# Five plain opening blocks for four, weights split ahead during the output product, and attention stacks in one step

## The chip, the cores and the metric

The kernel runs on one core of a Trainium2 chip, in one launch. The metric is device time in microseconds (us); a run's time is that of one execution, and a kernel's the median of its runs. The engines are called PE (TensorE, matmuls), DVE (VectorE), ACT (ScalarE), POOL (GpSimd) and SP (SyncE, which here issues the DMAs).

## The reference

An encoder trunk on x of 512 tokens by 1024 features, float32, two layers. Each layer is SwiGLU, a token mixer, SwiGLU, every one between two RMS norms:

```python
def swiglu(h, w_in, w_out):
    g, u = jnp.split(h @ w_in, 2, axis=-1)      # 1024 -> 2 x 2816
    return (jax.nn.silu(g) * u) @ w_out         # 2816 -> 1024

for layer in range(2):
    h = swiglu(rms_norm(x, g[0]), ffn_w_in[layer, 0], ffn_w_out[layer, 0])
    x = x + 0.5 * rms_norm(h, g[1])
    h = token_mixer(rms_norm(x, g[2]), ...)     # proj = h @ w_in; 8 attention heads of 64, 4 mLSTM heads of 128
    x = x + rms_norm(h, g[3])                   # mixer output: concat(heads) @ w_out
    h = swiglu(rms_norm(x, g[4]), ffn_w_in[layer, 1], ffn_w_out[layer, 1])
    x = x + 0.5 * rms_norm(h, g[5])
```

## The kernel before

All matmuls keep float32 accuracy with three products: each operand is a rounded part hi and a rest lo, and `hi*hi + hi*lo + lo*hi` is summed. Activations and weights are both split: ACT casts hi (L97, L114, L297), DVE subtracts to get lo (L99, L115, L299). Weights arrive by DMAs of 512 KB on SP's queue into a ring `raw` of three tiles; `hi` and `lo` are rings of three as well. A further set of numbered slots, reused over the whole program, holds activations and temporary tiles (`chunk(name, slot)`): 11 to 16 the tq pairs, 17 and 19 first the two xf tiles and later the loads `wu`, 18, 20 and 21 the weight sums `ws`.

**An FFN's input product** (`ffn_in`) goes over 22 column blocks f of 128. The first `ne` = 4 are plain openings, `block(f, left)` for tokens 0 to 255 and then `block(f, right)` for tokens 256 to 511, each loading and splitting the weights of g and u anew. So PE can work on the left half while the right half of the activations is still made. Then `xx.finish()` makes the last combined operand: it reads the tile xf in slot 17 and writes it split into the right half of xh and xl (L228 on ACT, L229 on DVE). From then on `seven(f)` computes a block for both halves with seven products in place of eight (Strassen-Winograd). It needs sums of weight quarters: `Weights(f)` loads g into the raw ring and u into slot 17 or 19 (`wu`, 17 + 2 * (f % 2); for f = ne + 1 the raw ring), DVE makes the sums (L320 to L323), ACT and DVE split them (L297, L299). PE's tiles there are pa, pb, pc.

**An output product** (`out_half`, for FFN and mixer) runs for tokens 0 to 255 and then 256 to 511 into tiles o; `whole` drives it. The FFN has 22 loads of weights in each half, the mixer 8. The last two blocks of a half are kept to its end. Behind each half, `chain(t)` follows for its two tiles of 128 tokens: `post` (L160; norm of the product and residual), `pre` (L174; next norm, nt at L185), PE transposes (tr, L191), the split into xh (L209) and xl (L210), and for an FFN the copies and sums that become xf and tq (L236 to L245, L228, L229). The powers for the norms are on POOL (L136). The chain of tokens 256 to 511 thus runs beside the start of the next stage.

**The mixer** begins with four groups of natural projections (`proj_nat`) on tiles 0 and 1, then transposed projections (`mixer_proj_T`), the groups again on tiles 2 and 3, gates, mLSTM, and attention. Attention takes 32 steps of scores (sc), softmax (sm) and transposes (pt); `stack_pair` puts a pair of heads into the layout that the scores need (PE stk, then kst, qsh and qsl by ACT and DVE), in two steps. It is paced with the first half of the output product.

Inside an engine, instructions run in program order; a scheduler that knows the dependences sets that order at build time from the order of the code. In the FFN's seven-product part the order is as written. The numbers behind tile names below are buffer numbers and only tell tiles of one name apart.

Of the kernel before, what the change touches and what calls it, by code (L numbers as in the profile page):

```python
# [18 lines left out]
P = 128  # L19
# [22 lines left out]
def trunk_kernel(ctx, tc, x, norm_gain, ffn_w_in, ffn_w_out, mix_w_in, conv_w, conv_b,  # L42
# [50 lines left out]

    def halves_of(src, n, after=None):
# [3 lines left out]
        with tc.issue_after(after) if after else nullcontext():  # L98
            V.tensor_tensor(lo[:, :n], src, hi[:, :n].bitcast(F32), ALU.subtract)  # L99
        return [[w[:, q: q + 512].rearrange("p (k c) -> p k c", k=4) for w in (hi, lo)] for q in range(0, n, 512)]  # L100

    def split_w(load, n, k4, pieces=1):
        raw = raw_tile()
        hi = wp.tile([P, 1056], F32R, tag="hi", name="hi", bufs=3)
        lo = wp.tile([P, 1056], F32R, tag="lo", name="lo", bufs=3)
        m = n * k4

        def view(w):
            return w[:, :m].rearrange("p (k c) -> p k c", k=k4)
        step = k4 // pieces  # L110
        for k in range(0, k4, step):
            r, h, l = [view(w)[:, k: k + step] for w in (raw, hi, lo)]
            load(r, k)
            A.copy(h, r)  # L114
            V.tensor_tensor(l, r, h.bitcast(F32), ALU.subtract)  # L115
        return view(hi), view(lo)
# [54 lines left out]

    first_nt = []

    def pre(t, xn, xx, ps_of):  # L174
        ss = small("pre_ss", 2)
        opening = len(first_nt) < 2
        if opening:
            V.tensor_tensor_reduce(out=xn[:, 512:1024], in0=xs[:, t, 512:1024], in1=xs[:, t, 512:1024], op0=ALU.mult,
                                   op1=ALU.add, scale=1.0, scalar=0.0, accum_out=ss[:, 1:2])
        for n in range(1 if opening else 2):  # L180
            A.activation(junk, xs[:, t, n * 512: n * 512 + 512], AF.Square, accum_out=ss[:, n: n + 1])
        r = rsqrt_sum((ss[:, 0:1], ss[:, 1:2]), D, EPS, "i")
        for hf in range(2):
            c = slice(hf * 512, hf * 512 + 512)
            V.scalar_tensor_tensor(xn[:, c], xs[:, t, c], r, gpre[:, c], ALU.mult, ALU.mult)  # L185
            if opening and hf:
                first_nt.append(last_ins(mybir.EngineType.DVE))
            ps = ps_of("tr")
            for k in range(4):
                kk = hf * 4 + k  # L190
                PE.transpose(ps[:, k * P: (k + 1) * P], xn[:, kk * P: (kk + 1) * P], ident)  # L191
            xx.put(t, hf, ps.rearrange("p (k c) -> p k c", k=4))
# [59 lines left out]
    def product(ps, w, x, start):  # L252
        (wh, wl), (xh, xl) = w, x
        for k in range(4):
            PE.matmul(ps, wh[:, k], xh[:, k], start=start and k == 0, stop=False, skip_group_check=True)  # L255
            PE.matmul(ps, wh[:, k], xl[:, k], start=False, stop=False, skip_group_check=True)  # L256
            PE.matmul(ps, wl[:, k], xh[:, k], start=False, stop=k == 3, skip_group_check=True)  # L257

    ps_even, ps_odd = banks_of(0, 1, 2), banks_of(4, 5, 6)

    def ffn_in(layer, j, xx, late=None):
        w = ffn_w_in[layer, j].rearrange("(k p) c -> p k c", p=P)
# [18 lines left out]

        def block(f, c, pieces=1, after=None):
            h = h_of(f) if hts[f] is None else hts[f]
            banks = []
            for gu in range(2):
                lo_k, hi_k = halves_of(load(f, gu, pieces, True)[:, :1024], 1024, after)
                ps = psA("gu")[:, c]
                for q, w2 in enumerate((lo_k, hi_k)):
                    product(ps, w2, [x[:, 4 * q: 4 * q + 4, c] for x in (xx.h, xx.l)], q == 0)
                banks.append(ps)  # L290
            sil = t2("sil", f % 2)[:, c]
            A.activation(sil, banks[0], AF.Silu)
            V.tensor_tensor(h[:, c], banks[1], sil, ALU.mult)
# [89 lines left out]

        ne = 4
        for f in range(ne):
            block(f, left, 2 if late and f == 0 else 1, first_nt[-1] if late and f == 0 else None)
            if late and f < 2:
                late[f]()
        for f in range(ne):
            block(f, right)  # L390
# [48 lines left out]

    def whole(gen):  # L440
        banks = next(gen)
        run(gen)
        return banks

    def ffn_out(layer, j, hts, last):
        w = ffn_w_out[layer, j]

        def lhs_of(half):
            def go(f, idx):
                src = hts[f][:, half * 256: half * 256 + 256]  # L450
# [6 lines left out]
        return [lambda h=h: whole(out_half(w, NF, range(NF), lhs_of(h), (psA, psB)[h], last and h == 1)) for h in range(2)]  # L457

# [25 lines left out]

    def proj_nat(layer, xx, col, n, evac, tiles=range(NT), ps_of=None, per=1):
        xh, xl = xx.h, xx.l
        w = mix_w_in[layer].rearrange("(k p) c -> p k c", p=P)
        parts = []
        for q in range(2):
            def load(dst, _, q=q):  # L490
                nc.sync.dma_start(dst, w[:, q * 4: q * 4 + 4, col: col + n])
            parts.append(split_w(load, n, 4))
        for t0 in tiles[::per]:
            ps = (ps_of or psA)("nat")
            for u in range(per):
                tok = slice((t0 + u) * P, (t0 + u + 1) * P)
                d = ps[:, u * n: (u + 1) * n]
                for k in range(NK):
                    wh, wl = parts[k // 4]
                    PE.matmul(d, xh[:, k, tok], wh[:, k % 4], start=k == 0, stop=False)  # L500
                    PE.matmul(d, xh[:, k, tok], wl[:, k % 4], start=False, stop=False)  # L501
                    PE.matmul(d, xl[:, k, tok], wh[:, k % 4], start=False, stop=k == NK - 1)  # L502
                    if k == 3:
                        yield
                if u == per - 1:
                    evac(t0, ps)
                yield
# [21 lines left out]

    def mixer(layer, xx):  # L530
        cwr = t2("cwr", 5)
# [40 lines left out]
        groups = ((3336, 264, evac_mo(1)), (2560, 256, evac_mv(0)), (2816, 256, evac_mv(1)), (3072, 264, evac_mo(0)))  # L572
        for n, g in enumerate(groups):
            run(proj_nat(layer, xx, *g, tiles=(0, 1), per=1 + (n in (1, 2))))
        qk = mixer_proj_T(layer, cvt, xx)
# [3 lines left out]
        for n, g in enumerate(groups[1:]):  # L579
            run(proj_nat(layer, xx, *g, tiles=(2, 3), per=1 + (n < 2)))  # L580
            if n == 1:
                with tc.issue_after(last_ins(mybir.EngineType.PE)):
                    gates = next(gates)
# [37 lines left out]
        def stack_pair(hp):  # L621
            base = (20, 4)[hp % 2]
            ks = pair("kst", base)
            stack(kn, hp, ks, None)
            yield
# [4 lines left out]
            yield  # L630

# [21 lines left out]
        def opening():  # L653
            for n, _ in enumerate(heads()):
                if n == 58:
                    run(stack_pair(0))
                if n in (60, 64):
# [6 lines left out]
        def lhs_of(half):  # L664
            def go(f, idx):
# [170 lines left out]
    def stack(src, hp, dh, dl):  # L836
# [9 lines left out]
        else:  # L846
            for e, s, o in ((0, lo, hi), (1, hi, lo)):
                A.copy(dh[s, e], ps[s])
                A.copy(dh[o, e], ps[s])
                V.tensor_tensor(dl[s, e], ps[s], dh[s, e].bitcast(F32), ALU.subtract)  # L850
                A.copy(dl[o, e], dl[s, e].bitcast(F32))

    def attention(stack_pair, stacks, pts, av, mask, mm):
# [157 lines left out]
```

## Time and profile before

| | |
|---|---|
| runs | 2122.14 us median of 3 (2122.1 to 2124.03) |
| profiled execution | 2122.1 us, its span 2120.1 us, granted TensorE clock 0.982 on average |
| busy PE / DVE / ACT / POOL | 2041.7 / 1544.4 / 1154.5 / 253.6 us |
| DMA | 270 MB, 127 GB/s on average |

The span is the time from the first to the last instruction. Busy time of PE is the union of its matmuls; a matmul begins before the last one has ended, so its own duration is longer than its cost. "Idle before" and the waits name what ended an engine's idle time.

### The profile page before, as it was taken

What the parts mean: (1) busy time and instruction counts of PE and PEld (TensorE: products, weight loads), DVE (VectorE), ACT (ScalarE), POOL (GpSimd) and SP (SyncE); (2) the same over time, 40 slices, a digit from 0 to 9 for tenths busy, and PEclk for the clock granted to TensorE, in tenths of its full rate; (3) what the DMA queues carried; (4) which work ended last, traced back from release to release, by engine and by line L of the source; (5) the groups of instructions that cost most, each with busy time, mean ns of one, the idle gap of its engine ahead of it and who ended that gap; (6) DMA issues with size and microseconds to landing.
All of it is one profiled execution on the core that took longest, in us unless ns stands there. A gap on an engine that the chain in (4) does not pass through costs nothing. (4 is left out here: it accounts for less than half of the span.)

```text
span 2120.1 us, 35561 instructions
## 1 busy us (share of the span) xinstructions
PE 2041.7 (96%) x13870; PEld 1861.2 (88%) x13870; DVE 1544.4 (73%) x2634; ACT 1154.5 (54%) x2058; POOL 253.6 (12%) x330
## 2 busy tenths in 40 slices
PE   8899999999999989999998999999999999899998
PEld 7899988889977889998898999888899779899886
DVE  7688757685767878876687886667856677788665
ACT  5455555445665645555554555554456755455554
POOL 1000001233512100000010000003434220000000
PEclk9999999999999999999999999999999999999999
DMA  7433355541113633335663334564411235333364
GB/s 217 123 111 100 110 188 193 143 122 58 53 51 119 190 110 107 113 102 187 188 188 107 105 100 129 188 192 126 119 53 41 88 122 160 110 104 115 120 205 144
DMA packets 297566, 270.28 MB, mean 127 GB/s; under 512 B 8661, under 2 KB 267189, under 8 KB 297398
## 3 DMA queue, kind: packets, MB, share of 16 engines
q1 hardware_dynamic: 297398, 268.01, 41.8%
q8 instruction: 108, 1.77, 0.3%
q14 instruction: 60, 0.49, 0.1%
HBM read 265.88 MB, written 2.10 MB: 126 GB/s over the span
## 5 line engine op out<-in xcount | busy, mean ns | idle before, releaser
L115 DVE TENSOR_TENSOR lo<-raw,hi 128x1024 fp32r<-128x1024 f32 (+1 forms) x280 | 348.8, 1246 | 241.4 <-ACT hi L114 241.3
L114 ACT CAST hi<-raw 128x1024 fp32r<-128x1024 f32 (+1 forms) x280 | 294.5, 1053 | 311.0 <-PE o L419 225.6
L417 PE MATMUL o<-lo,hq 128*128 128x512 f32 x704 | 236.9, 394 | 0.8 <-DVE lo L115 0.8
L419 PE MATMUL o<-hi,hq 128*128 128x512 f32 x704 | 223.3, 394 | 0.0
L416 PE MATMUL o<-hi,hq 128*128 128x512 f32 x704 | 210.6, 395 | 2.5 <-ACT hq L453 2.5
L297 ACT CAST hi<-ws 128x1024 fp32r<-128x1024 f32 x144 | 151.2, 1052 | 70.9 <-ACT a L297 62.1
L255 PE MATMUL pa<-tq,hi 128*128 128x256 f32 x576 | 164.6, 286 | 22.3 <-ACT hi L297 22.3
L500 PE MATMUL nat<-hi,xh 128*128 128x256 f32 (+1 forms) x640 | 184.9, 291 | 0.0
L501 PE MATMUL nat<-lo,xh 128*128 128x256 f32 (+1 forms) x640 | 182.0, 285 | 2.9 <-DVE lo L115 2.9
L502 PE MATMUL nat<-hi,xl 128*128 128x256 f32 (+1 forms) x640 | 181.6, 285 | 0.0
L299 DVE TENSOR_TENSOR lo<-ws,hi 128x1024 fp32r<-128x1024 f32 x144 | 175.2, 1219 | 1.5 <-ACT hi L297 1.5
L257 PE MATMUL pa<-tq,lo 128*128 128x256 f32 x576 | 165.0, 286 | 1.9 <-DVE lo L299 1.9
L256 PE MATMUL pa<-tq,hi 128*128 128x256 f32 x576 | 164.8, 286 | 0.0
L255 PE MATMUL pc<-xh,hi 128*128 128x256 f32 x576 | 163.6, 284 | 0.0
L257 PE MATMUL pc<-xh,lo 128*128 128x256 f32 x576 | 163.4, 284 | 0.0
L256 PE MATMUL pc<-xl,hi 128*128 128x256 f32 x576 | 163.4, 284 | 0.0
L416 PEld LDWEIGHTS o<-hi,hq 128*128 128x128 f32 x704 | 131.9, 188 | 34.0 <-ACT hq L453 3.4
L417 PEld LDWEIGHTS o<-lo,hq 128*128 128x128 f32 x704 | 131.9, 188 | 31.5 <-DVE lo L115 1.1
L419 PEld LDWEIGHTS o<-hi,hq 128*128 128x128 f32 x704 | 132.3, 188 | 30.8
L256 PE MATMUL gu<-xl,hi 128*128 128x256 f32 x512 | 147.4, 289 | 6.6 <-DVE xl L210 6.6
L255 PE MATMUL gu<-xh,hi 128*128 128x256 f32 x512 | 146.8, 290 | 4.6 <-ACT xf L236 3.7
L257 PE MATMUL gu<-xh,lo 128*128 128x256 f32 x512 | 146.3, 288 | 0.0
(242 smaller groups left out, 5660.3 us busy)
## 6 DMA issues: line engine op xcount, KB each, us to landing
raw<-in_ffn_w_out_dram SPq DMA_DIRECT2D x176, 512.0 KB, 3.5
raw<-in_ffn_w_in_dram SPq DMA_DIRECT2D x138, 512.0 KB, 3.9
wu<-in_ffn_w_in_dram SPq DMA_DIRECT2D x68, 512.0 KB, 4.0
raw<-in_mix_w_in_dram SPq DMA_DIRECT2D x56, 512.0 KB, 3.8
raw<-in_mix_w_out_dram SPq DMA_DIRECT2D x32, 512.0 KB, 3.7
raw<-in_mix_w_in_dram SPq DMA_DIRECT2D x16, 528.0 KB, 3.7
gpost<-in_norm_gain_dram SPq DMA_DIRECT2D x6, 512.0 KB, 5.9
gpre<-in_norm_gain_dram SPq DMA_DIRECT2D x5, 512.0 KB, 4.7
```

Of the source, the lines that this page charges most:

```text
L114: A.copy(h, r)
L115: V.tensor_tensor(l, r, h.bitcast(F32), ALU.subtract)
L255: PE.matmul(ps, wh[:, k], xh[:, k], start=start and k == 0, stop=False, skip_group_check=True)
L256: PE.matmul(ps, wh[:, k], xl[:, k], start=False, stop=False, skip_group_check=True)
L257: PE.matmul(ps, wl[:, k], xh[:, k], start=False, stop=k == 3, skip_group_check=True)
L299: V.tensor_tensor(lo, src, fp(hi), ALU.subtract)
L416: PE.matmul(banks[t][n], a, wh[:, n], start=first, stop=False)
L417: PE.matmul(banks[t][n], a, wl[:, n], start=False, stop=False)
L419: PE.matmul(banks[t][n], b, wh[:, n], start=False, stop=end)
L500: PE.matmul(d, xh[:, k, tok], wh[:, k % 4], start=k == 0, stop=False)
L501: PE.matmul(d, xh[:, k, tok], wl[:, k % 4], start=False, stop=False)
L502: PE.matmul(d, xl[:, k, tok], wh[:, k % 4], start=False, stop=k == NK - 1)
```

## The change

- `ffn_in` has five plain openings. The right pass goes backwards (4, 3, 2, 1, 0), and the split weights of f = 4 are kept from the left pass to the right pass, which saves one load and split of g and u. The first seven-product block is f = 5.
- `early_split` loads and splits weights of the next stage while the second half of an output product runs, into slots 11 to 16, 20 and 21, which are free then. Ahead of three of the four FFNs these are g and u of f = 0 and 1 (four splits), ahead of each mixer the two parts of column group 2560 (two splits): 16 in all. `whole` calls them at even distances.
- In the mixer's first four groups, group 2560 comes first, and the second lo of the three other groups is subtracted on POOL.
- `stack_pair` runs in one step, at score steps 3, 13 and 17 in place of 2/4, 9/11 and 16/18. The second half of qsl is made by DVE from PSUM, no longer copied by ACT.
- At the opening of the kernel both squares of a norm are on ACT, and the rule that put the second nt ahead of the first lo is gone.
- The second half of the gates is taken one group later in the code; the order of instructions around it is the same.

The program has 48 matmuls more (128x256 each), 12 fewer lo subtracts of weights on DVE in the FFN input products (without the early ones), and as many DMAs as before.

The first place is the end of the right pass in the third FFN, ACT. `sil` ends an opening block, `xh<-xf` is the finish, `a22` and `hi<-ws` are casts of wu and of the weight sums, `ha` and `sil` wait for PE. Before:

```order
L297 CAST hi_12127<-raw_12117 128x1024
L292 ACTIVATE sil_12112<-gu_12056 128x256
L228 CAST xh_10437<-xf_10439 128x4x256
L350 COPY ha_12149<-pa_12152 128x256
L297 CAST a22_12136<-wu_12119 128x512
```

Now:

```order
L320 ACTIVATE sil_12152<-gu_12096 128x256
L325 CAST hi_12232<-raw_12222 128x1024
L325 CAST hi_12235<-ws_12226 128x1024
L320 ACTIVATE sil_12217<-gu_12161 128x256
L219 CAST xh_10423<-xf_10425 128x4x256
L325 CAST hi_12238<-ws_12227 128x1024
L378 COPY ha_12253<-pa_12256 128x256
```

The first `hi<-ws` moved from behind the finish and the first pa to a place ahead of the finish, and the finish no longer stands ahead of anything that reads wu.

The second place is SP's queue during the second half of the first layer's mixer output product. `raw<-in_mix_w_out` are its own weights, `raw<-in_ffn_w_in` those of the FFN that follows. Before:

```order
L423 DMA raw_7383<-in_mix_w_out_dram 128x1024
L423 DMA raw_7401<-in_mix_w_out_dram 128x1024
L423 DMA raw_7419<-in_mix_w_out_dram 128x1024
L423 DMA raw_7437<-in_mix_w_out_dram 128x1024
L423 DMA raw_7455<-in_mix_w_out_dram 128x1024
L423 DMA raw_7473<-in_mix_w_out_dram 128x1024
L423 DMA raw_7491<-in_mix_w_out_dram 128x1024
L423 DMA raw_7497<-in_mix_w_out_dram 128x1024
L272 DMA raw_7648<-in_ffn_w_in_dram 128x8x128
```

Now:

```order
L451 DMA raw_7376<-in_mix_w_out_dram 128x1024
L451 DMA raw_7394<-in_mix_w_out_dram 128x1024
L267 DMA raw_7412<-in_ffn_w_in_dram 128x8x128
L451 DMA raw_7418<-in_mix_w_out_dram 128x1024
L451 DMA raw_7436<-in_mix_w_out_dram 128x1024
L267 DMA raw_7448<-in_ffn_w_in_dram 128x8x128
L451 DMA raw_7460<-in_mix_w_out_dram 128x1024
L267 DMA raw_7478<-in_ffn_w_in_dram 128x8x128
L451 DMA raw_7484<-in_mix_w_out_dram 128x1024
L451 DMA raw_7502<-in_mix_w_out_dram 128x1024
L451 DMA raw_7508<-in_mix_w_out_dram 128x1024
L267 DMA raw_7520<-in_ffn_w_in_dram 128x8x128
```

Four early loads (L267) stand among the eight, three of them ahead of the last; all go through the same ring of three raw tiles.

The third place is PE in the first layer's attention, where the last pair of heads is stacked (`stk<-qn`) and its first score (sc) follows. Before:

```order
L839 MATMUL stk_6843<-idj_73,qn_5149 128x128 x2
L839 MATMUL stk_6843<-idj_73,qn_5150 128x128 x2
L870 MATMUL sc_6907<-kst_6787,qsh_6841 128x512
L886 MATMUL pt_6917<-idj_73,sm_6834 128x128 x4
L871 MATMUL sc_6907<-kst_6787,qsl_6842 128x512
```

Now:

```order
L872 MATMUL stk_6808<-idj_73,qn_5142 128x128 x2
L872 MATMUL stk_6808<-idj_73,qn_5143 128x128 x2
L919 MATMUL pt_6882<-idj_73,sm_6789 128x128 x4
L444 MATMUL o_6766<-hi_6939,mrg_5619 128x512
L445 MATMUL o_6766<-lo_6940,mrg_5619 128x512
L444 MATMUL o_6767<-hi_6939,mrg_5619 128x512
L445 MATMUL o_6767<-lo_6940,mrg_5619 128x512
L447 MATMUL o_6766<-hi_6939,mrg_5619 128x512
L447 MATMUL o_6767<-hi_6939,mrg_5619 128x512
L919 MATMUL pt_6910<-idj_73,sm_6842 128x128 x4
L903 MATMUL sc_6900<-kst_6796,qsh_6806 128x512
```

The score of the new pair no longer stands directly behind its stack.

The core of the diff:

```diff
     def pre(t, xn, xx, ps_of):
         ss = small("pre_ss", 2)
-        opening = len(first_nt) < 2
-        if opening:
-            V.tensor_tensor_reduce(out=xn[:, 512:1024], in0=xs[:, t, 512:1024], in1=xs[:, t, 512:1024], op0=ALU.mult,
-                                   op1=ALU.add, scale=1.0, scalar=0.0, accum_out=ss[:, 1:2])
-        for n in range(1 if opening else 2):
+        for n in range(2):
             A.activation(junk, xs[:, t, n * 512: n * 512 + 512], AF.Square, accum_out=ss[:, n: n + 1])
...
+    def early_split(made, key, slots, load, cols):
+        raw = raw_tile()
+        load(raw)
+        hi, lo = [chunk("early", q, F32R)[:, :1024] for q in slots]
+        A.copy(hi, raw[:, :1024])
+        V.tensor_tensor(lo, raw[:, :1024], fp(hi), ALU.subtract)
+        made[key] = [[w[:, q: q + cols * 4].rearrange("p (k c) -> p k c", k=4) for w in (hi, lo)]
+                     for q in range(0, 1024, cols * 4)]
...
             for gu in range(2):
-                lo_k, hi_k = halves_of(load(f, gu, pieces, True)[:, :1024], 1024, after)
+                if (f, gu) in made:
+                    lo_k, hi_k = made.pop((f, gu))
+                else:
+                    lo_k, hi_k = halves_of(load(f, gu, pieces, True)[:, :1024], 1024)
+                if c is left and f == ne - 1:
+                    made[f, gu] = lo_k, hi_k
...
-        ne = 4
+        ne = 5
         for f in range(ne):
...
-        for f in range(ne):
+        for f in reversed(range(ne)):
             block(f, right)
...
-    def whole(gen):
+    def whole(gen, nf, fill=()):
         banks = next(gen)
-        run(gen)
+        fill = list(fill)
+        for n, _ in enumerate(gen):
+            if fill and n >= 2 * nf * (5 - len(fill)) // 5:
+                fill.pop(0)()
         return banks
...
-        for n, g in enumerate(groups):
-            run(proj_nat(layer, xx, *g, tiles=(0, 1), per=1 + (n in (1, 2))))
+        for n in (1, 0, 2, 3):
+            run(proj_nat(layer, xx, *groups[n], tiles=(0, 1), sub=G, per=1 + (n in (1, 2)), made=made))
...
-                A.copy(dl[o, e], dl[s, e].bitcast(F32))
+                V.tensor_tensor(dl[o, e], ps[s], dh[s, e].bitcast(F32), ALU.subtract)
...
-                if n in (2, 9, 16):
-                    made = stack_pair(1 + n // 7)
-                if n in (2, 4, 9, 11, 16, 18):
-                    next(made)
+                if n in (3, 13, 17):
+                    stack_pair((3, 13, 17).index(n) + 1)
...
+            made, early = ({}, ()) if last else mixer_early(nl) if nsub == 1 else ffn_early(nl, nsub // 2)
             for h in range(2):
-                banks = halves[h]()
+                banks = halves[h](early if h else ())
```

More of the change, by code (lines that the diff above doesn't have):

```diff
@@ L92, in raw_tile, with halves_of @@
         return wp.tile([P, 1056], F32, tag="raw", name="raw", bufs=3)
-    def halves_of(src, n, after=None):
+    def halves_of(src, n):
         hi = wp.tile([P, 1056], F32R, tag="hi", name="hi", bufs=3)
@@ L97, in halves_of, with split_w @@
         A.copy(hi[:, :n], src)
-        with tc.issue_after(after) if after else nullcontext():
-            V.tensor_tensor(lo[:, :n], src, hi[:, :n].bitcast(F32), ALU.subtract)
+        V.tensor_tensor(lo[:, :n], src, hi[:, :n].bitcast(F32), ALU.subtract)
         return [[w[:, q: q + 512].rearrange("p (k c) -> p k c", k=4) for w in (hi, lo)] for q in range(0, n, 512)]
-    def split_w(load, n, k4, pieces=1):
+    def split_w(load, n, k4, sub=None, pieces=1):
         raw = raw_tile()
@@ L114, in split_w @@
             A.copy(h, r)
-            V.tensor_tensor(l, r, h.bitcast(F32), ALU.subtract)
+            (sub or V).tensor_tensor(l, r, h.bitcast(F32), ALU.subtract)
         return view(hi), view(lo)
@@ L170, in post @@
             V.scalar_tensor_tensor(xs[:, t, c], y[:, c], r, xs[:, t, c], ALU.mult, ALU.add)
-    first_nt = []
     def pre(t, xn, xx, ps_of):
         ss = small("pre_ss", 2)
-        opening = len(first_nt) < 2
-        if opening:
-            V.tensor_tensor_reduce(out=xn[:, 512:1024], in0=xs[:, t, 512:1024], in1=xs[:, t, 512:1024], op0=ALU.mult,
-                                   op1=ALU.add, scale=1.0, scalar=0.0, accum_out=ss[:, 1:2])
-        for n in range(1 if opening else 2):
+        for n in range(2):
             A.activation(junk, xs[:, t, n * 512: n * 512 + 512], AF.Square, accum_out=ss[:, n: n + 1])
@@ L185, in pre @@
             V.scalar_tensor_tensor(xn[:, c], xs[:, t, c], r, gpre[:, c], ALU.mult, ALU.mult)
-            if opening and hf:
-                first_nt.append(last_ins(mybir.EngineType.DVE))
             ps = ps_of("tr")
@@ L257, in product, with ffn_early, step, load @@
             PE.matmul(ps, wl[:, k], xh[:, k], start=False, stop=k == 3, skip_group_check=True)
+    def early_split(made, key, slots, load, cols):
[6 more added lines that the diff above has]
+                     for q in range(0, 1024, cols * 4)]
+    def ffn_early(layer, j):
+        w = ffn_w_in[layer, j].rearrange("(k p) c -> p k c", p=P)
+        made = {}
+        def step(f, gu):
+            def load(raw):
+                col = gu * FF + f * P
+                nc.sync.dma_start(raw[:, :1024].rearrange("p (k c) -> p k c", k=NK), w[:, :, col: col + P])
+            slots = ((11, 12, 13, 14), (15, 16, 20, 21))[f][2 * gu: 2 * gu + 2]
+            return lambda: early_split(made, (f, gu), slots, load, P)
+        return made, [step(f, gu) for f in range(2) for gu in range(2)]
+    def mixer_early(layer):
+        w = mix_w_in[layer].rearrange("(k p) c -> p k c", p=P)
+        made = {}
+        def step(q):
+            def load(raw):
+                nc.sync.dma_start(raw[:, :1024].rearrange("p (k c) -> p k c", k=4), w[:, q * 4: q * 4 + 4, 2560: 2816])
+            return lambda: early_split(made, q, (11 + 2 * q, 12 + 2 * q), load, 256)
+        return made, [step(q) for q in range(2)]
     ps_even, ps_odd = banks_of(0, 1, 2), banks_of(4, 5, 6)
-    def ffn_in(layer, j, xx, late=None):
+    def ffn_in(layer, j, xx, made, late=None):
         w = ffn_w_in[layer, j].rearrange("(k p) c -> p k c", p=P)
@@ L280, in h_of, with block @@
             return hts[f]
-        def block(f, c, pieces=1, after=None):
+        def block(f, c, pieces=1):
             h = h_of(f) if hts[f] is None else hts[f]
@@ L382, in seven @@
             V.tensor_tensor(h[:, right], u1, g1, ALU.mult)
-        ne = 4
+        ne = 5
         for f in range(ne):
-            block(f, left, 2 if late and f == 0 else 1, first_nt[-1] if late and f == 0 else None)
+            block(f, left, 2 if late and f == 0 else 1)
             if late and f < 2:
                 late[f]()
-        for f in range(ne):
+        for f in reversed(range(ne)):
             block(f, right)
@@ L456, in lhs_of @@
             return go
-        return [lambda h=h: whole(out_half(w, NF, range(NF), lhs_of(h), (psA, psB)[h], last and h == 1)) for h in range(2)]
+        return [lambda fill=(), h=h: whole(out_half(w, NF, range(NF), lhs_of(h), (psA, psB)[h], last and h == 1), NF, fill)
+                for h in range(2)]
     def mixer_proj_T(layer, cvt, xx):
@@ L483, in mixer_proj_T, with proj_nat @@
         return qk
-    def proj_nat(layer, xx, col, n, evac, tiles=range(NT), ps_of=None, per=1):
+    def proj_nat(layer, xx, col, n, evac, tiles=range(NT), ps_of=None, sub=None, per=1, made=None):
         xh, xl = xx.h, xx.l
@@ L491, in load @@
                 nc.sync.dma_start(dst, w[:, q * 4: q * 4 + 4, col: col + n])
-            parts.append(split_w(load, n, 4))
+            if made and q in made:
+                parts.append(made.pop(q)[0])
+            else:
+                parts.append(split_w(load, n, 4, sub if q else None))
         for t0 in tiles[::per]:
@@ L528, in take, with mixer @@
                 yield
-    def mixer(layer, xx):
+    def mixer(layer, xx, made):
         cwr = t2("cwr", 5)
@@ L580, in mixer @@
             run(proj_nat(layer, xx, *g, tiles=(2, 3), per=1 + (n < 2)))
-            if n == 1:
+            if n == 2:
                 with tc.issue_after(last_ins(mybir.EngineType.PE)):
@@ L624, in stack_pair @@
             stack(kn, hp, ks, None)
-            yield
             qh = pair("qsh", base + 1)
@@ L629, in stack_pair @@
             stacks[hp] = (ks, qh, ql)
-            yield
         def projections():
@@ L655, in opening @@
                 if n == 58:
-                    run(stack_pair(0))
+                    stack_pair(0)
                 if n in (60, 64):
@@ L670, in mixer @@
         paced(att, 19, gen, 16, 2)
-        return [lambda: banks,
-                lambda: whole(out_half(mix_w_out[layer], NK, (4, 5, 6, 7, 0, 1, 2, 3), lhs_of(1), psB))]
+        return [lambda fill=(): banks,
+                lambda fill=(): whole(out_half(mix_w_out[layer], NK, (4, 5, 6, 7, 0, 1, 2, 3), lhs_of(1), psB), NK, fill)]
     def mixer_gates(gt):
@@ L949, in trunk_kernel @@
     late = [lambda: start(2), lambda: start(3)]
+    made = {}
     for layer in range(DEPTH):
@@ L954, in trunk_kernel @@
             if sub == 1:
-                halves = mixer(layer, xx)
+                halves = mixer(layer, xx, made)
             else:
-                halves = ffn_out(layer, sub // 2, ffn_in(layer, sub // 2, xx, late), last)
+                halves = ffn_out(layer, sub // 2, ffn_in(layer, sub // 2, xx, made, late), last)
                 late = None
```

## The prediction

> **What bounds the kernel now.** I read the busy line first, then the chain of waits of the tensor engine, then its granted clock in the stretches behind the long waits, and last the timeline of each place. All durations are from one execution of 2122.1 us (span 2120.1 and 2.0 around it); the median of the runs is 2122.14, so the sum may stand against either.
>
> ```profile
> PE 2041.7 (96%) x13870; PEld 1861.2 (88%) x13870; DVE 1544.4 (73%) x2634; ACT 1154.5 (54%) x2058; POOL 253.6 (12%) x330
> ```
>
> PE is the bound for 96% of the span: every matmul added is paid in full, and a saving can only come from the 78 us in which PE sits idle, or from matmuls that run slower than they could. Who ends the idle time:
>
> ```profile
> PE pa L255 <- ACT hi L297: 22.3, 4, 5.7
> PE tr L191 <- DVE nt L185: 12.4, 6, 4.3
> PE gu L256 <- DVE xl L210: 6.6, 2, 3.6
> PE sc L870 <- ACT qsh L849: 3.9, 4, 1.3
> PE gu L255 <- ACT xf L236: 3.7, 1, 3.7
> PE pa L257 <- DVE lo L299: 1.9, 4, 0.5
> PE projT L120 <- DVE xl L210: 1.3, 2, 0.9
> PE gu L255 <- ACT xh L209: 0.9, 2, 0.7
> PE sc L871 <- ACT qsl L851: 0.9, 2, 0.4
> ```
>
> The columns are total us, number of waits, longest. The first and sixth row are one place in each of the four FFNs: the first seven-product block. The second row holds three kinds: the opening (its longest, 4.3), the right pass of the FFN that follows an FFN (3.9, row below) and the two mixer starts (the remaining 4.2, rows below). The third and eighth are the right passes behind the two mixers.
>
> These idle times cost more than they show. The stretches below are 8 us long and begin where PE resumes; the number in brackets behind PE is its matmuls, and the column before the last two is the granted clock.
>
> ```profile
> 75.90:83.90 8.00, 7.49 (x43) 7.19 (x44) 5.86 (x8) 4.42 (x7) 0.00 (x0) 0.66 0.59 169
> 725.90:733.90 8.00, 8.00 (x54) 8.00 (x55) 6.96 (x11) 4.51 (x7) 0.39 (x1) 0.79 0.48 140
> 758.60:766.60 8.00, 7.52 (x43) 7.23 (x44) 5.89 (x8) 4.39 (x7) 0.00 (x0) 0.67 0.56 164
> 1090.60:1098.60 8.00, 8.00 (x52) 7.49 (x53) 7.12 (x10) 4.29 (x7) 1.28 (x1) 0.79 0.55 182
> 1124.80:1132.80 8.00, 7.53 (x47) 7.24 (x48) 6.29 (x8) 4.36 (x7) 0.00 (x0) 0.73 0.58 170
> 1774.90:1782.90 8.00, 7.96 (x44) 7.96 (x45) 5.75 (x10) 3.73 (x6) 0.00 (x0) 0.61 0.46 134
> 1808.60:1816.60 8.00, 7.51 (x38) 7.22 (x39) 5.39 (x6) 4.12 (x7) 0.00 (x0) 0.58 0.58 168
> 628.00:636.00 8.00, 7.68 (x30) 4.87 (x31) 2.49 (x6) 2.55 (x6) 0.69 (x1) 0.61 0.01 3
> 1456.00:1464.00 8.00, 7.34 (x27) 5.52 (x28) 3.08 (x4) 0.96 (x2) 0.80 (x1) 0.79 0.25 73
> 1676.60:1684.60 8.00, 6.88 (x34) 4.35 (x33) 2.96 (x7) 4.07 (x8) 0.84 (x2) 0.79 0.14 56
> ```
>
> PE counts as busy there, but on 0.58 to 0.79 of its clock: after a few us of idleness the clock is lowered for some us. The pace at full clock:
>
> ```profile
> 1062.87 0.28 PE L255 MATMUL gu<-xh,hi 128*128 128x256 f32 x1
> ...
> 1063.93 0.28 PE L255 MATMUL gu<-xh,hi 128*128 128x256 f32 x1
> ```
>
> The second is the ninth after the first: 1.06 / 9 = 0.118 us from start to start (the 0.28 overlaps the next and is no cost), so 68 in 8 us; a matmul on 512 columns is then 0.236. The four stretches behind the pa wait (first, third, fifth, seventh) have 43, 43, 47 and 38: 101 short, 11.9 us, of which about 0.5 each is the pa L257 wait itself. That leaves **10 us** of slow clock. The three at the right passes (54, 52, 44) lack 54 matmuls, or by the clock 8 x (0.21 + 0.21 + 0.39) = 6.5 us; I take **6**.
>
> **The change, part by part.**
>
> *Five openings for four: the price.* A plain block is 2 passes x 2 (g, u) x 8 slices x 3 terms = 96 matmuls, a seven-product block 7 x 4 x 3 = 84; so 12 more in each FFN, 48 x 0.118 = **+5.7 us**. At the row's 0.28 each it would be 13.4, the upper end.
>
> *The first seven-product block.* The end of the third FFN's right pass:
>
> ```profile
> 1114.92 1.05 ACT L228 CAST xh<-xf 128x1024 fp32r<-128x1024 f32 x1 [1.03 <-PE gu L257]
> 1116.01 1.23 DVE L229 TENSOR_TENSOR xl<-xf,xh 128x1024 fp32r<-128x1024 f32 x1 [3.13 <-ACT xh L228]
> 1117.26 6.18 SPq L272 DMA_DIRECT2D wu<-in_ffn_w_in_dram  x2
> 1121.15 0.62 ACT L297 CAST a<-wu 128x512 fp32r<-128x512 f32 x1 [3.02 <-DMA wu<-in_ffn_w_in_dram]
> 1123.69 1.99 ACT L297 CAST hi<-ws 128x1024 fp32r<-128x1024 f32 x2 [1.91 <-DVE ws L322]
> 1124.78 0.58 PE L255 MATMUL pa<-tq,hi 128*128 128x256 f32 x1 [5.65 <-ACT hi L297]
> ```
>
> `finish` reads the tile xf in slot 17; the load of wu goes into the same slot, so it is issued at 1117.26, right behind L229, lands at about 1121.1, and sums, cast and pa follow. With five openings the first such wu belongs to f = 5 and goes to slot 19, whose last readers are the sums that form tq when the right half is transposed, a whole right pass earlier, and f = 6 loads into the raw ring; nothing waits for `finish`. In the new order the cast of the first sums stands two places ahead of the finish on ACT (excerpt above). Next late is the second cast, behind the finish: from the pass's end 0.4 for sil, 1.05 (L228), 1.05 for the cast, so ready about 2.5 us after, while PE has 24 matmuls (pa, pb: 2.8 us) and the tq product (1.4) to do first. Both rows, 22.3 + 1.9 = 24.2, go but for some 0.7: **-23.5**, and with them the slow clock behind them, **-10**.
>
> *Early splits: the right passes.* The chain of tiles 2 and 3 (post, pre, transposes) shares DVE with the splits of the left pass, and PE reaches the right pass before nt or xl:
>
> ```profile
> 1090.58 0.66 PE L191 MATMUL tr<-idj,nt 128*128 128x128 f32 x4 [3.94 <-DVE nt L185]
> 725.89 0.39 PE L256 MATMUL gu<-xl,hi 128*128 128x256 f32 x1 [3.01 <-DVE xl L210]
> ```
>
> Now the left pass is a fifth block longer (48 matmuls, 5.7 us) and has four splits less on DVE (4 x 1.2). PE comes 5.7 us later to something that is some 5 us earlier; the waits are under 4. They go: 3.9 + 6.6 + 0.9 = **-11.4**, and **-6** of slow clock. The reversed right pass begins on the kept weights, so that no load stands at its start. Should DVE hand the time to other work, half stays: +9.
>
> *Early splits: what they cost.* Sixteen DMAs, casts and subtracts move into the output products. An FFN's half is 22 x 12 x 0.236 = 62 us for 22 loads; four more add 4 x 1.2 to DVE, which is idle for a quarter of the span. The mixer's second half is short: 8 loads in 8 x 12 x 0.236 = 22.7 us, and now 12, on SP's queue between the others (excerpt above).
>
> ```profile
> 680.62 1.22 DVE L115 TENSOR_TENSOR lo<-raw,hi 128x1024 fp32r<-128x1024 f32 x1 [1.26 <-ACT hi L114]
> 689.56 1.23 DVE L115 TENSOR_TENSOR lo<-raw,hi 128x1024 fp32r<-128x1024 f32 x1
> 685.60 1.05 ACT L114 CAST hi<-raw 128x1024 fp32r<-128x1024 f32 x1 [0.92 <-DMA raw<-in_mix_w_out_dram]
> 688.48 1.05 ACT L114 CAST hi<-raw 128x1024 fp32r<-128x1024 f32 x1 [0.86 <-DMA raw<-in_mix_w_out_dram]
> 696.39 0.40 PE L255 MATMUL gu<-xh,hi 128*128 128x256 f32 x2
> raw<-in_mix_w_out_dram SPq DMA_DIRECT2D x32, 512.0 KB, 3.7
> ```
>
> Both casts wait for their DMA already, and the last lo is ready at 690.8, where the closing products of the half begin (24 matmuls of 0.236 before the next stage at 696.39). A load's way through the ring of three is 3.7 + 1.05 + 1.22 = 6.0 us, 2 us for each load; two early ones stand ahead of the last loads with about 1 us of slack: late by 3. I take **+6** for both layers (bounds 0 and 2 x 6), with **+2** for a slow clock behind one of them and **+1** for the FFN halves.
>
> *Mixer start.* Group 2560 first, with its weights split early, and six subtracts to POOL. What waits:
>
> ```profile
> 1455.10 0.66 PE L191 MATMUL tr<-idj,nt 128*128 128x128 f32 x4 [1.59 <-DVE nt L185]
> L810 POOL TENSOR_TENSOR hs<-hs,den 128x1024 f32<-128x1024 f32 x8 | 15.2, 1898 | 2.3 <-DVE den L808 1.9
> 688.01 1.42 DVE L185 SCALAR_TENSOR_TENSOR nt<-xs,rs_yi,gpre 128x512 f32<-128x512 f32 x2
> 404.64 1.12 DVE L185 SCALAR_TENSOR_TENSOR nt<-xs,rs_yi,gpre 128x512 f32<-128x512 f32 x1
> ```
>
> tr (4.2) and projT (1.3) are 5.5 in both layers. DVE loses 2 early and 3 POOL subtracts, 6 us, ahead of the last nt, so it goes, by the same reasoning as at the right passes. Against it: POOL takes 1.9 us for this form (L810), in order ahead of its rs powers, which the chain needs; and a DVE operation beside POOL is slower (L185: 1.12 for one, against 1.42 for two). Three such stretches of 0.4 are about 1 us: **-4.5**, with **-0.8** of the 8 x 0.21 of slow clock at 1456. Bounds: -7.2 and +6 (three POOL lo's of 1.9 in series with the chain).
>
> This is where the Trainium skill speaks against the change: by "SBUF — State Buffer", Who interferes with whom, a VectorE instruction with two SBUF inputs and a GpSimd instruction that reads SBUF exclude one another for a whole instruction. The rows show a slowing of 0.4, not a full block of 1.9; by the rule the mixer starts would give 6 x 1.9 = 11.4 us back, less what no chain waits for.
>
> *Attention.* The stack of a pair in one step, and the second half of qsl straight from PSUM on DVE instead of by ACT from the first. The two sc rows are 4.8 us. In the new order two transposes of four and six o matmuls on 512 columns (8 x 0.118 + 6 x 0.236 = 2.4 us; excerpt above) stand between a stack and its first score, more than the longest wait of 1.3. **-3** (bounds 0 and -4.8), and half of the 8 x (0.39 + 0.21) of slow clock, **-2.5**; half only, since PE also waits for softmax there. DVE's extra 16 x 0.69 us lie in a stage where it is half idle.
>
> *Opening.* Two squares go from DVE to ACT, and the order that put the second nt ahead of the first lo's is gone: that nt may come 2 x 1.2 later, while the first comes earlier. The gu L255 wait of 3.7 then moves by **+0.4** (bounds -0.5 and +2).
>
> Gates, tail and the initial loads stay.
>
> **Sum:** +5.7 - 23.5 - 10 - 11.4 - 6 + 6 + 2 + 1 - 5.3 - 5.5 + 0.4 = -46.6, so 2122.1 - 46.6 = 2075.5; I forecast **2075 us**.
>
> **Rivals.**
> 1. *The mixer's output half becomes the wait.* If the ring gives no slack, each of three early loads ahead of the last costs its 2 us, and the clock falls behind it (1.7): 7.7 a layer for 4 assumed, +7.4, 2083. For: two casts there wait for DMA already. Against: the early halves have tiles of their own, so they do not hold the hi and lo rings.
> 2. *The clock stays low.* A wait of 1.59 us was enough at 1456; if waits of 1 to 2 us are left at the old places, the 19.3 us credited to the clock (10, 6, 0.8, 2.5) stay: 2095.
> 3. *POOL against DVE.* Each POOL subtract keeps DVE out for its whole 1.9 us instead of slowing it: 6 x 1.9 = 11.4 for the 1 that is in the sum, 2085. For it: L185 is slower beside POOL; against it: by 0.4 only.
> 4. *The change doesn't do what it says:* the wait at the first seven-product block stays, because ACT does the finish first or raw for f = 6 comes late. +33.5: 2109. Against it is the order on ACT.
> 5. *Slower.* Each early split holds an output product for its whole way, 6.0 us: 16 x 6.0 = 96. The credits are 61.7 (23.5, 10, 11.4, 6, 5.3, 5.5), less 5.7 for the matmuls 56: 2122 - 56 + 96 = 2162. It decides from 56 / 16 = 3.5 us for each split. Against: one split in each 12 matmuls' 2.8 us passes there already, and DVE idles before the lo at 680.62.
>
> **Chances.** Forecast (2067 to 2082) 0.5; first rival 0.17, second 0.1, third 0.1, fourth 0.08 (0.03 of it joined by the first two: 2109 + 9 + 7 = 2125, no change), fifth 0.03, and 0.02 below 2067. The range runs from 2064, where mixer start and attention come out at their lower ends (-2.7, -1.8) and the output halves cost nothing (-8), to 2097, just past the second rival; it leaves out the fourth and fifth. What a measurement can tell is 0.2%, 4.2 us: faster 0.94, same 0.03, slower 0.03.
>
> **What would show it.** After: no pa row over 1 us, and a clock of 1.00 behind it; tr and gu L256 rows down to the opening's; 48 matmuls more; a new row of o waiting for lo or hi in the mixer's second output half, 3 us a layer; sc rows near 1. I am wrong if the pa wait survives under another releaser, or o waits for its weights by more than 6 us a layer.

## The result, and the profile after

The changed kernel takes 2070.64 us (median of 4 runs, 2067.55 to 2071.91) against 2122.12: a ratio of 0.9754, 95% interval 0.9737 to 0.9771, or 51.5 us less. Forecast were 2075 us, 47 less, in a range of 2064 to 2097. The busy line and the waits of the tensor engine after (columns as in the prediction):

```profile
span 2068.6 us, 35581 instructions
PE 2027.4 (98%) x13918; PEld 1849.4 (89%) x13918; DVE 1533.8 (74%) x2604; ACT 1132.3 (55%) x2026; POOL 258.1 (12%) x336
```

```profile
PE tr L182 <- DVE nt L178: 10.5, 4, 5.7
PE gnat L760 <- DVE gates L754: 5.4, 4, 1.6
PE pt L919 <- ACT pts L924: 3.6, 6, 0.9
...
PE po L935 <- DVE qsl L884: 2.6, 2, 1.3
...
PE nat L536 <- POOL lo L114: 0.6, 2, 0.3
PE sc L903 <- ACT qsh L882: 0.5, 2, 0.2
PE pt L919 <- POOL sm L912: 0.4, 1, 0.4
```

One row of the attention before, for comparison:

```profile
PE pt L886 <- POOL sm L879: 2.7, 4, 0.9
```

The pa rows are gone, and so are the gu rows behind the mixers. Of the 10.5 us of tr, 2.75 are the two mixer starts (1.38 and 1.37), the rest is the opening. The score wait went from 4.8 to 0.5, but two new rows, pt waiting for pts and po waiting for qsl, have 6.2 between them. With the wait for softmax (sm), which fell from 2.7 to 0.4, these rows of the attention have 7.5 before and 7.1 after: the waits moved and hardly shrank. PE is busy for 14.3 us less although it has 48 matmuls more: the clock. The stretches of 8 us that answer to those of before, from the first matmul of a seven-product part and of a right pass, show it:

```profile
710.40:718.40 8.00, 8.00 (x71) 8.00 (x70) 8.00 (x12) 5.74 (x10) 1.04 (x1) 1.00 0.87 253
747.80:755.80 8.00, 8.00 (x70) 8.00 (x69) 7.22 (x11) 5.01 (x8) 0.00 (x0) 1.00 0.48 140
1063.10:1071.10 8.00, 8.00 (x71) 8.00 (x70) 8.00 (x13) 5.59 (x10) 1.05 (x1) 1.00 0.71 191
1100.60:1108.60 8.00, 8.00 (x70) 8.00 (x69) 7.25 (x11) 5.00 (x8) 0.00 (x0) 1.00 0.36 105
1643.10:1651.10 8.00, 6.77 (x32) 4.62 (x33) 3.00 (x9) 1.94 (x4) 0.69 (x1) 0.79 0.00 0
```

70 or 71 matmuls in place of 38 to 54, at a clock of 1.00. Lowered stretches are left in the attention of the second layer (last row) and at the gates of both layers, behind the gnat waits of 5.4 us, where the kernel before had them too:

```profile
479.40:487.40 8.00, 7.58 (x46) 7.49 (x47) 0.00 (x0) 4.17 (x20) 1.17 (x4) 0.68 0.35 109
1499.70:1507.70 8.00, 7.61 (x46) 7.51 (x47) 0.00 (x0) 4.17 (x20) 1.17 (x4) 0.66 0.32 103
```

Where the time went, by the starts of the first matmuls of each part in the two timelines (us):

| part | before | after | difference |
|---|---|---|---|
| to the first gu | 17.8 | 18.3 | +0.5 |
| opening blocks, FFN 1 | 49.7 | 61.3 | +11.6 |
| first pa to the first projT | 339.9 | 322.3 | -17.6 |
| projT to gu of FFN 2 | 289.0 | 287.2 | -1.8 |
| opening blocks, FFN 2 | 53.5 | 58.7 | +5.2 |
| pa of FFN 2 to pa of FFN 3 | 366.3 | 352.8 | -13.5 |
| pa of FFN 3 to the second projT | 340.5 | 321.5 | -19.0 |
| projT to gu of FFN 4 | 288.9 | 287.4 | -1.5 |
| opening blocks, FFN 4 | 54.6 | 58.7 | +4.1 |
| pa of FFN 4 to the end | 320.0 | 300.5 | -19.5 |

A further plain block adds 96 x 0.118 = 11.3 and takes a seven-product block away, 84 x 0.118 = 9.9. So the right passes behind the mixers gained 11.3 - 5.2 = 6.1 and 11.3 - 4.1 = 7.2, and the last seven-product part 19.5 - 9.9 = 9.6.

### The profile page after: what moved, and what is told of

Same layout as the page of the kernel before. It is cut to its first block, busy times and chain, and to the rows that moved or that the text cites. A ratio compares the mean times of both kernels' runs of the same rounds, so it can differ in the third digit from the quotient of the medians.

```text
span 2068.6 us, 35581 instructions
## 1 busy us (share of the span) xinstructions
PE 2027.4 (98%) x13918; PEld 1849.4 (89%) x13918; DVE 1533.8 (74%) x2604; ACT 1132.3 (55%) x2026; POOL 258.1 (12%) x336
## 4 chain that ended last, share of the span: by engine, by line
PE 90%; DVE 5%; issue 2%; ACT 2%; DMA 1%; POOL 0%; SPq 0%; DVEq 0%; POOLq 0%; ACTq 0%
PE o L444 9%; PE o L445 9%; PE o L447 9%; PE pa L247 6%; PE pa L248 6%; PE pa L246 6%; PE gu L247 4%; PE gu L246 4%; PE gu L248 4%; PE pc L248 3%; PE pc L247 3%; PE pc L246 3%; PE nat L535 2%; PE nat L536 2%; PE nat L537 2%
## 5 line engine op out<-in xcount | busy, mean ns | idle before, releaser
L114 DVE TENSOR_TENSOR lo<-raw,hi 128x1024 fp32r<-128x1024 f32 (+1 forms) x270 | 337.0, 1249 | 211.0 <-ACT hi L113 210.1
L536 PE MATMUL nat<-lo,xh 128*128 128x256 f32 (+1 forms) x608 | 173.2, 286 | 2.9 <-DVE lo L114 2.4
L535 PE MATMUL nat<-hi,xh 128*128 128x256 f32 (+1 forms) x608 | 175.9, 291 | 0.0
L537 PE MATMUL nat<-hi,xl 128*128 128x256 f32 (+1 forms) x608 | 172.7, 285 | 0.0
L327 DVE TENSOR_TENSOR lo<-ws,hi 128x1024 fp32r<-128x1024 f32 x136 | 165.9, 1220 | 4.5 <-ACT hi L325 4.3
L247 PE MATMUL pa<-tq,hi 128*128 128x256 f32 x544 | 153.2, 282 | 0.0
L248 PE MATMUL pc<-xh,lo 128*128 128x256 f32 x544 | 153.1, 281 | 0.0
L248 PE MATMUL pa<-tq,lo 128*128 128x256 f32 x544 | 153.1, 281 | 0.0
L247 PE MATMUL pc<-xl,hi 128*128 128x256 f32 x544 | 152.9, 281 | 0.0
L246 PE MATMUL pc<-xh,hi 128*128 128x256 f32 x544 | 152.8, 281 | 0.0
L246 PE MATMUL pa<-tq,hi 128*128 128x256 f32 x544 | 152.6, 281 | 0.0
```

The source lines that it names most:

```text
L114: (sub or V).tensor_tensor(l, r, h.bitcast(F32), ALU.subtract)
```

## The experiments

Each is an edit of the changed kernel unless the text says otherwise; e1 to e11 are the names of the runs.

**The slot of wu.** In `e1_slot17` (e1):

```diff
-            raw = chunk("wu", 17 + 2 * (f % 2)) if gu and not whole_f else raw_tile()
+            raw = chunk("wu", 17 + 2 * ((f + 1) % 2)) if gu and not whole_f else raw_tile()
```

> The changed kernel with one edit: the load wu of block f goes into slot 17 + 2 * ((f + 1) % 2), so that u of f = 5, the first seven-product block, lands in slot 17 again, which the finish reads. Five openings, early splits and all else stay. Theory (slot reuse): the load waits for the finish as before the change, so the pa wait is back in four places, 24.2 us of idle PE and about 10 us of slow clock behind them: 2071 + 34 = 2105. Rival (the fifth opening itself, its longer right pass and kept weights, gave the time): the wait stays away, 2071 to 2075.

Measured 2107.36 us (ratio to the kernel before 0.9934, 0.9919 to 0.9949). With five openings and all early splits, the pa waits are those of the kernel before; tr stays as in the changed kernel, and no gu row comes back:

```profile
PE pa L246 <- ACT hi L325: 22.6, 4, 5.7
PE tr L182 <- DVE nt L178: 9.9, 4, 5.2
...
PE pa L248 <- DVE lo L327: 1.9, 4, 0.5
```

The reverse (e6): the same one-line edit in the kernel before, which has four openings, so that u of f = 4 goes to slot 19.

> The kernel before with only the slots of wu swapped: u of f = 4 to slot 19, four openings, nothing else changed. Theory (slot reuse): the pa wait (24.2 us) and the slow clock behind it (10 us) go: 2122 - 34 = 2088. Rival (something behind the load is late as well, such as the raw ring or the casts behind the finish on ACT): half or less of it, 2105 to 2120.

Measured 2086.31 us (0.9836, 0.9821 to 0.9850), 35.1 less than before in the same session (2121.44). No pa row is left; tr, gu and sc stay as they were:

```profile
PE tr L191 <- DVE nt L185: 11.7, 6, 4.1
PE gu L256 <- DVE xl L210: 6.3, 2, 3.6
...
PE sc L870 <- ACT qsh L849: 3.9, 4, 1.3
```

So two thirds of the change's gain is the parity of a slot number. The fifth opening gave it only because it made the first wu one with odd f.

**What covers the right pass.** Four openings with the slots swapped, all else as changed (e2):

```diff
+            raw = chunk("wu", 17 + 2 * ((f + 1) % 2)) if gu and not whole_f else raw_tile()
...
-        ne = 5
+        ne = 4
```

> The changed kernel with four openings and the slots of wu swapped, so that u of f = 4 goes to slot 19. Theory (slot reuse, and early splits enough for the right passes): the first seven-product block does not wait, 48 matmuls of 0.118 us are saved, and the right pass begins 5.7 us earlier where the changed kernel's trace leaves 5.0 us between the last xl (1067.3) and the pass (about 1072.3): waits under 1 us. 2071 - 5.7 + 2 = 2067. Rival (the fifth block is what covers the chain): the waits at three right passes come back, 11.4 us with 6 us of slow clock: 2071 - 5.7 + 17.4 = 2083.

Measured 2063.74 us (0.9731, 0.9715 to 0.9747), 6.9 less than the changed kernel. The 48 matmuls are 5.7 of it by their pace; in the two profiles 1.0 more lies ahead of the first gu (17.3 against 18.3), where the kernels are alike. The timeline of the third FFN shows how close it is; the last xl and PE at the start of the right pass, about 1061:

```profile
1059.90 0.68 DVE L201 TENSOR_TENSOR xl<-tr,xh 128x512 fp32r<-128x512 f32 x1
```

```profile
1060.81 0.29 PE L248 MATMUL gu<-xh,lo 128*128 128x256 f32 x1
1060.93 0.52 PE L246 MATMUL gu<-xh,hi 128*128 128x256 f32 x3
1061.29 0.28 PE L247 MATMUL gu<-xl,hi 128*128 128x256 f32 x1
```

The other way round, five openings and no early split (e3):

```diff
-            made, early = ({}, ()) if last else mixer_early(nl) if nsub == 1 else ffn_early(nl, nsub // 2)
+            made, early = {}, ()
```

> The changed kernel without early splits (all sixteen are done where their product is). Theory (the fifth block covers the chain): in the kernel before, the chain was late by 3.9 us; 5.7 us more of left pass against 2 more splits on DVE (2.4 us) leave it 0.6 late at most, so the right passes cost 0 to 2 us, the mixer starts give back their 3: 2071 + 4 = 2075. Rival (the early splits cover it): waits of about 4 us at three right passes with slow clock, +17: 2088.

Measured 2072.71 us (0.9771, 0.9756 to 0.9786): 2 us more than with sixteen early splits, which the intervals do not tell from nothing. Neither of the right passes' rows (tr 3.9, gu 3.0) came back; the largest wait there is 0.24 us. Then neither a fifth block nor early splits (e7: four openings, slot 19, the edit of e3):

> Four openings, u of f = 4 in slot 19, and no early splits. Theory (either a fifth block or the early splits cover the chain of tokens 256 to 511, and without both its waits are back): the kernel with early splits took 2064; waits of about 3.7 us at three right passes and 6 us of slow clock: 2064 + 17 = 2081. Rival (the kept weights at the turn to the backward right pass, one load and two splits less, cover it): 2064 to 2070.

Measured 2074.83 us (0.9781, 0.9767 to 0.9794), 11 more than with early splits and less than the theory's 17. The waits at the three right passes are back, but at 1.4 to 1.5 us each and not 3.7. By the stages of the two profiles 8.1 of the time lies there (opening blocks of FFN 2 and FFN 4 2.3 and 3.4, pa of FFN 2 to pa of FFN 3 2.4), most of the rest behind projT. A likely reason for the shorter waits is the backward turn on kept weights, which takes two splits off DVE; no run has it alone.

```profile
PE tr L182 <- DVE nt L178: 12.6, 11, 4.9
...
PE gu L247 <- DVE xl L201: 2.9, 2, 1.5
```

Three openings with early splits (e8), the slot rule as in the changed kernel (f = 3 is odd):

```diff
-        ne = 5
+        ne = 3
```

> Three openings with early splits, the first u of the seven-product blocks (f = 3) in slot 19. Theory (the left pass must last until the last xl): with four openings the right pass of the third FFN begins 0.5 us after the last xl (1060.5 against 1061.0), so 5.7 us less of left pass leaves waits of 4 to 5 us at three right passes with slow clock behind them (6): 2064 - 5.7 + 13.5 + 6 = 2078. Rival (the order of DVE gives the chain the freed time): 2064 - 5.7 = 2058.

Measured 2077.84 us (0.9787, 0.9773 to 0.9800), as the theory has it: three blocks are too short for the chain, four just long enough. Behind the mixers PE waits 2.95 for nt and 1.45 for xl, 4.4 as expected; in the third FFN only 0.86 and 1.45.

```profile
PE tr L182 <- DVE nt L178: 16.5, 7, 4.9
...
PE gu L247 <- DVE xl L201: 4.3, 3, 1.5
```

**The stacks.** The two-step stacks of the kernel before, at steps 2/4, 9/11, 16/18, with ACT's copy of qsl (e4; the two `yield`s that make `stack_pair` two steps again are left out here):

```diff
...
-                V.tensor_tensor(dl[o, e], ps[s], dh[s, e].bitcast(F32), ALU.subtract)
+                A.copy(dl[o, e], dl[s, e].bitcast(F32))
...
-                if n in (3, 13, 17):
-                    stack_pair((3, 13, 17).index(n) + 1)
+                if n in (2, 9, 16):
+                    made = stack_pair(1 + n // 7)
+                if n in (2, 4, 9, 11, 16, 18):
+                    next(made)
```

> The changed kernel with the stacks as before (two steps, at score steps 2/4, 9/11, 16/18; second half of qsl copied by ACT). Theory (the wait moved): the score waits come back (about 4.5 us) and the waits for pts and qsl that took their place (3.6 and 2.6 us) go; idle PE in the mixer behind its projections was 8.2 us before and after, so 2071, within 2. Rival (the stacks are worth what was forecast): 2071 + 5.5 = 2076.

Measured 2068.43 us (0.9751, 0.9738 to 0.9764): not distinguishable from the changed kernel (0.9737 to 0.9771). The score waits and the wait for softmax are back, the wait for pts is down from 3.6 to 0.8, and po no longer waits for qsl:

```profile
PE sc L905 <- ACT qsh L884: 3.9, 4, 1.3
PE pt L921 <- POOL sm L914: 2.7, 4, 0.9
...
PE sc L906 <- ACT qsl L886: 0.9, 2, 0.4
PE pt L921 <- ACT pts L926: 0.8, 2, 0.4
```

**POOL's subtracts.** All lo subtracts of the weights on DVE (e5):

```diff
-            run(proj_nat(layer, xx, *groups[n], tiles=(0, 1), sub=G, per=1 + (n in (1, 2)), made=made))
+            run(proj_nat(layer, xx, *groups[n], tiles=(0, 1), per=1 + (n in (1, 2)), made=made))
```

> The changed kernel with all lo subtracts on DVE, none on POOL. Theory (POOL takes work off the chain): three subtracts of 1.2 us are ahead of the last nt of each mixer again, so the tr wait of 1.4 us grows by up to 3.7 us in both layers: 2071 + 4 = 2075 (up to 2078). Rival (a POOL subtract keeps DVE out for its whole 1.9 us): without them DVE is freed, 2071 - 4 = 2067. Second rival: no chain waits for either, 2071.

Measured 2062.51 us (0.9722, 0.9708 to 0.9735): 8 us faster without them: the first rival, and further than it had it. By stages, pa to projT went from 322.3 to 319.6 and from 321.5 to 318.9, so about 2.65 in each mixer start; about 1 us lies in the opening, whose start was between 17.0 and 18.3 in kernels that are alike there. What the subtracts do is seen in the first mixer's start of the changed kernel. POOL first, then DVE:

```profile
386.28 2.37 POOL L114 TENSOR_TENSOR lo<-raw,hi 128x1024 fp32r<-128x1024 f32 x1
...
393.44 2.46 POOL L114 TENSOR_TENSOR lo<-raw,hi 128x1056 fp32r<-128x1056 f32 x1
```

```profile
386.25 0.16 DVE L592 TENSOR_TENSOR gt<-nat,gb 128x16 f32<-128x16 f32 x1
386.36 2.30 DVE L138 SCALAR_TENSOR_TENSOR rs_yo<-rs_ao,rs_yo 128x1 f32<-128x1 f32 x1
...
393.61 2.31 DVE L137 SCALAR_TENSOR_TENSOR rs_ai<-rs_yi,rs_vi 128x1 f32<-128x1 f32 x1
```

and DVE at the same two operations without the subtracts:

```profile
386.10 0.15 DVE L138 SCALAR_TENSOR_TENSOR rs_yo<-rs_ao,rs_yo 128x1 f32<-128x1 f32 x1
...
391.61 0.22 DVE L137 SCALAR_TENSOR_TENSOR rs_ai<-rs_yi,rs_vi 128x1 f32<-128x1 f32 x1 [0.48 <-POOL rs_yi L135]
```

An operation on one column takes 2.30 us and ends when POOL ends (388.65); without POOL it takes 0.15. It stands as busy time of DVE, not as a wait. Both are on the chain of the last nt, for which PE then waits 1.38. The third subtract, from 374.68 to 377.15, holds an `rs_uo` further ahead for 0.63, which takes 0.15 in e5. The Trainium skill's "SBUF — State Buffer", Who interferes with whom, says just this: a VectorE instruction with two SBUF inputs and a GpSimd instruction that reads SBUF exclude each other for the whole instruction. The trace agrees, 2.30 against 2.37.

**Together.** Four openings, slot 19, no POOL subtracts (e9):

> Four openings with u of f = 4 in slot 19, early splits, and all lo subtracts on DVE. Theory (the two gains are of different places and add): 2071 less 7 for the fifth opening (2064 measured) less 5.3 for the two mixer starts (2.65 each by the stages of the trace without POOL subtracts): 2058. Rival (the longer left pass or the POOL subtracts served something that the other had covered): 2062 or more.

Measured 2059.20 us (0.9709, 0.9694 to 0.9724), the fastest: 62.7 under the kernel before in its session, and 11.4 under the median of the changed one, which was taken in another. The tr row is the opening alone:

```profile
PE tr L182 <- DVE nt L178: 6.8, 2, 5.1
```

The same without the mixer's early splits (e10; `mixer_early` is not called):

> The same (four openings, slot 19, no POOL subtracts) with early splits ahead of the FFNs alone, twelve in place of sixteen; group 2560 still comes first in the mixer. Theory (the mixer's early splits cover nothing that PE waits for): 2058, within 2. Rival (they keep DVE free for the last nt): two splits of 1.2 us and their loads are back in each mixer start, 2058 + 5 = 2063.

Measured 2065.48 us (0.9740, 0.9724 to 0.9757), the rival. Of the 6.3 us, 4.0 lie between pa and projT (329.4 to 331.8, and 329.6 to 331.2), where the waits of the kernel before are back:

```profile
PE tr L182 <- DVE nt L178: 10.4, 6, 4.4
...
PE projT L119 <- DVE xl L201: 1.9, 2, 0.9
```

And e9 with the old stacks (e11):

> Four openings, slot 19, no POOL subtracts, sixteen early splits, and the stacks of the kernel before. Theory (the one-step stacks only move the wait): 2058, 1 less to 1 more. Rival (they are worth their score waits where the rest is faster): 2063.

Measured 2060.42 us (0.9716, 0.9701 to 0.9732): 1.2 us, which the intervals do not tell from nothing.

## Why the prediction was right, and where it was not

The time was 4 us under the forecast, and the two large terms held. But three smaller steps were wrong and nearly cancelled: +9 for the early splits came to nothing, -5.3 at the mixer start came to nothing, and of -5.5 in the attention at most 3.3 came (all that projT to gu gained in both layers). So 9 too much stood against 7.5 to 10.8 too little; that the sum came so close is in this part luck.

- *Matmuls, +5.7.* The two kernels that differ by the fifth block are 6.9 apart (e2), of which 1.0 lies ahead of the blocks. Right; the 0.28 of the row would have given 13.4.
- *First seven-product block, -23.5 and -10 of clock.* Taking it back alone cost 36.7 (e1, 2107.36 - 2070.64), giving it alone to the kernel before saved 35.1 (e6). Right in mechanism and size. The idle time alone, 24.5, would have left 10 to 12 us unexplained. The load of wu is issued at 1074.73, 26 us ahead of the first pa, and the second cast, the last of the rows of ACT, is done at 1101.8, 1.6 us before PE reaches the tq product:

```profile
1074.73 0.37 SPq L295 DMA_DIRECT2D wu<-in_ffn_w_in_dram  x1
```

```profile
1097.91 1.05 ACT L325 CAST hi<-ws 128x1024 fp32r<-128x1024 f32 x1 [1.85 <-PE gu L247]
...
1099.41 1.05 ACT L219 CAST xh<-xf 128x1024 fp32r<-128x1024 f32 x1 [0.17 <-PE gu L248]
1100.75 1.05 ACT L325 CAST hi<-ws 128x1024 fp32r<-128x1024 f32 x1 [0.29 <-PE gu L247]
```

```profile
1103.45 0.28 PE L246 MATMUL pa<-tq,hi 128*128 128x256 f32 x1
```

- *Right passes, -11.4 and -6.* Behind the mixers they gained 6.1 and 7.2; the third was counted with its neighbours. For it stand e6 and e2, both with four openings and slot 19: pa of FFN 2 to pa of FFN 3 takes 356.8 and 351.4, so 5.4. Right in size, 18.7 for 17.4. But the step added two covers, a longer left pass and a freed DVE, where either is enough (e2, e3); with neither, waits of 1.4 us return (e7). Beside the fifth block the sixteen early splits gave nothing that can be told (e3).
- *Cost of the early splits, +9.* Wrong: no new o row for weights appeared, and projT to gu did not grow (-1.8, -1.5). The step took the lateness as 3 and the slack as 1. The last lo of the mixer's half is ready 3.8 us before the next stage (684.16 + 1.23 against 689.15), 5.6 before (690.79 against 696.39): late by 1.8. And it is not needed where the closing products begin, since those of the block before it come first: in the kernel's order the last four of the eight products with lo in the closing part read it. The first of these four, the last row below, starts 1.9 us after it is ready:

```profile
683.08 1.05 ACT L113 CAST hi<-raw 128x1024 fp32r<-128x1024 f32 x1 [1.05 <-DMA raw<-in_mix_w_out_dram]
```

```profile
684.16 1.23 DVE L114 TENSOR_TENSOR lo<-raw,hi 128x1024 fp32r<-128x1024 f32 x1 [0.88 <-ACT hi L113]
```

```profile
687.31 0.39 PE L445 MATMUL o<-lo,mrg 128*128 128x512 f32 x1
```

  So there is no wait, and 1.9 us are still in hand. In the kernel before, the last lo (ready at 690.79) is first read by this row, so the slack there was 3.0 and not 1:

```profile
693.78 0.47 PE L417 MATMUL o<-lo,mrg 128*128 128x512 f32 x1
```

- *Mixer start, -4.5 and -0.8.* Wrong step: "three such stretches of 0.4 are about 1 us". From one operation beside a short POOL instruction I took the price of a partial slowing; DVE stands still for all of POOL's 2.4 us, and that cost 2.65 in each layer (e5). It was the third rival, whose chance of 0.1 was too low, though its 10 us were too much: of three subtracts a layer, two held an operation of the chain for nearly their whole length and the third one for 0.63. As a whole the step gave nothing: e6, with the mixer start of the kernel before, has 331.7 and 332.2 from pa to projT, less 9.9 for one seven-product block 321.8 and 322.3; the changed kernel has 322.3 and 321.5. Without POOL's subtracts it is 319.6 and 318.9 (e5), together 5.6 less than e6, so the early splits gave what was forecast for the whole step (e10 confirms it, 4.0), and POOL took it back.
- *Attention, -3 and -2.5.* Wrong: 1.2 at best (e11), and e4 shows nothing. The distance from stack to score was read rightly and the score wait fell to 0.5, but waits for pts and for the next qsl took its place, and both are made by the engines that make the stack. e4 and e11 turn back the single step, its places and DVE's share of qsl together, so which of the three moved the wait is open. The step asked only who waits for the stack, not what else those engines had to deliver.
- *Opening, +0.4.* +0.5 here, and between -0.8 and +0.5 in kernels with the same opening: not resolved.

The second rival (a slow clock that stays) and the slower one are refuted by the profile: the granted clock went from 0.982 to 0.995 on average, and no output product waits for an early split. Not settled is why e10 is also slower than e9 between projT and gu, by 2.8 and 1.7 in their profiles, part of which it regains elsewhere. The lower end of the range is 1 us above its own working (2075.5 - 2.7 - 1.8 - 8 = 2063).

## What to carry to other kernels

When a load waits for the last reader of its buffer, look first whether another buffer of the same size is free by then: here one changed parity gave 35 of 63 us, and the extra work that came with the same effect was not needed. Price idle time of the tensor engine with the matmuls behind it, which ran at a lowered clock for 3.4 us or longer (8 x 0.21 lost at half of it; from 1092 to 1095 of the kernel before the granted clock reads 0.50): 24.5 us of idle time cost 35 to 37 here. Moving work to a helper engine was no gain here, since its instructions held up the engine that they were to relieve; look at that engine's small operations, where the block shows as a long duration and not as a wait.

## What the runs showed of the hardware that was not expected

A DVE operation on 128x1 elements with two inputs took 2.30 and 2.31 us while a POOL subtract of 2.37 and 2.46 us ran, against 0.15 and 0.22 alone: a full block and not a sharing. Not every operation is held: two `nt<-o,gpost` at 375.21, which read o from PSUM, took 1.41 us beside the third subtract and 1.28 without it (e5).
